# Where the row work of the last matrix product runs: three moves in the tail of a hybrid decoder block on one Trainium2 core

## The chip, the cores and the metric

The kernel runs on one core of a Trainium2 chip. The metric is device time in microseconds (us) of one execution; three executions of the kernel before gave 1152.98, 1154.11 and 1154.29, median 1154.11. Engine names are those of the profile: PE multiplies matrices, DVE and ACT work on elements and rows, POOL is the general-purpose engine (GpSimd), and SP only issues DMA transfers here.

## The reference

One decoder layer in float32 on 1024 tokens of width 1024. Everything but the last two lines is left alone by the change:

```python
n = _rmsnorm(h, pre_mix_gain[l])
...                                     # two groups of heads, mixed into h
h = h + _rmsnorm(mix, post_mix_gain[l])
n2 = _rmsnorm(h, pre_ffn_gain[l])
gu = jnp.einsum('bsd,df->bsf', n2, w_ffn_in[l])
ff = jax.nn.silu(gu[..., :D_FF]) * gu[..., D_FF:]
ff = jnp.einsum('bsf,fd->bsd', ff, w_ffn_out[l])      # the down product, D_FF = 2816
h = h + _rmsnorm(ff, post_ffn_gain[l])                # the row work
```

The row work of a token is the sum of squares of its 1024 results, one reciprocal root from it, and `h + ff * root * gain`.

## The kernel before, in words

The last stage, the down product, multiplies 2816 inner values for 1024 tokens and 1024 columns. It is cut into halves both ways (a Strassen-like scheme), so that seven half-size products take the place of eight. They run in the order p = 1, 2, 6, 5, 7, 3, 4. Each goes through 11 steps j (`NJ`), each step through four token tiles i of 128, and each tile takes three matmuls of 128x512, because float32 values are split into a high and a low part: `dah`/`dal` for the activations, `dwh`/`dwl` for the weights (`mm3`, lines 118 to 120). One step is 12 matmuls.

While step n runs, the operands of step n+4 (`AHEAD`) are prepared. `down_load` lets SP load 128x512 of weights (`dwr`) and of activations (`dar`), 256 KB each. `down_split` makes the high part on ACT (line 114) and the low part on DVE (line 115), for both. All of these tiles have four buffers. The high part of step n+4 is written where that of step n stood, so ACT waits until PE is through with n; and the load of `dar` for n+4 goes where that of n stood, so it waits for the DVE's subtraction of n.

The product's results come in tiles of 128 tokens by 512 columns. `PAIRS` names four pairs of token tiles (t0, t1); pair i keeps its partial results in `parts`: c11 and c12 are the two column halves of t0, c22 the second half of t1, and the first half of t1 is what the PSUM bank dA holds after p = 4. c11 is complete after p = 2, c22 after p = 7, c12 after p = 3.

The row work stands in three helpers. `row_tiles` loads the 128x1024 rows of h (`ht`, 512 KB). `square` sums the squares of a half on ACT and multiplies it by the gain into `y`. `ffn_tail` gets the root through DVE and POOL (`rstd2`, lines 100 and 102), adds `y` times root to `ht` on DVE (line 1149, two halves), and lets SP store each half (line 1151). All of it is written in p = 4. The t0 tiles of the pairs stand in steps 0 to 3, with the gain multiplication on POOL; the rows of t1 are loaded in steps 3 to 6 into the four buffers that t0 used.

The last four steps of p = 4 (`late`) are turned round: tile by tile, steps 7 to 10 of it, so that the tiles of t1 come to an end one after the other, and each one's row work follows (`after`).

The program's text does not fix where an instruction stands on its engine. A scheduler places instructions by when it expects them to be ready, for each engine, and the engine then takes them strictly in that order. SP's queue is such an order too: a transfer that waits holds up the ones behind it.

Of the kernel before, what the change touches and what calls it, by code (L numbers as in the profile page):

```python
# [7 lines left out]
F32 = mybir.dt.float32  # L8
F32R = mybir.dt.float32r
AF = mybir.ActivationFunctionType  # L10
ALU = mybir.AluOpType
PSUM = bass.MemoryType.PSUM

P = 128
S = 1024
D = 1024
NT = S // P
# [12 lines left out]
PAIRS = [(0, 6), (1, 7), (2, 4), (3, 5)]  # L30
# [18 lines left out]
def hybrid_block(ctx: ExitStack, tc: tile.TileContext, io: dict, out: bass.AP):  # L49
# [1081 lines left out]
    def row_tiles(t):  # L1131
        ht = po.tile([P, D], F32, tag="ht", name=f"ht_{t}", bufs=4)
        nc.sync.dma_start(out=ht, in_=h_d[t * P:(t + 1) * P, :])
        rows[t] = ht, small(2, "sq"), po.tile([P, D], F32, tag="y", name=f"y_{t}", bufs=4)

    def square(t, dh, src, eng):
        ht, ss, y = rows[t]
        cs = slice(dh * 512, dh * 512 + 512)
        s = po.tile([P, 512], F32, tag="junk", name=f"junk_{t}_{dh}", bufs=2)
        nc.scalar.activation(s, src, AF.Square, scale=D ** -0.5, accum_out=ss[:, dh:dh + 1])  # L1140
        eng.tensor_tensor(out=y[:, cs], in0=src, in1=gpo[:, cs], op=ALU.mult)  # L1141

    def ffn_tail(t):
        ht, ss, y = rows[t]
        ts = slice(t * P, (t + 1) * P)
        r = rstd2(ss)
        for dh in range(2):
            cs = slice(dh * 512, dh * 512 + 512)
            nc.vector.scalar_tensor_tensor(out=ht[:, cs], in0=y[:, cs], scalar=r, in1=ht[:, cs],
                                           op0=ALU.mult, op1=ALU.add)  # L1150
            nc.sync.dma_start(out=out[ts, cs], in_=ht[:, cs])
# [6 lines left out]
    def after(p, i):  # L1158
# [14 lines left out]
        elif p == 3:  # L1173
            nc.vector.tensor_tensor(out=parts["c12", i], in0=c, in1=parts["c12", i], op=ALU.add)
        else:
            square(t1, 0, a, nc.vector)
            ffn_tail(t1)
# [4 lines left out]
    for p in (1, 2, 6, 5, 7, 3, 4):  # L1182
# [4 lines left out]
        if p == 4:  # L1187
            for i in range(4):
                row_tiles(PAIRS[i][0])
        late = range(NJ - 4, NJ) if p == 4 else range(0)  # L1190
        for j in range(NJ):
# [11 lines left out]
            if p == 4 and j < 4:  # L1203
                t0, t1 = PAIRS[j]
                for dh in range(2):
                    square(t0, dh, parts[("c11", "c12")[dh], j], nc.gpsimd)
                ffn_tail(t0)
            if p == 4 and 3 <= j < 7:
                t1 = PAIRS[j - 3][1]
                row_tiles(t1)  # L1210
                square(t1, 1, parts["c22", j - 3], nc.gpsimd)
# [48 lines left out]
```

## Time and profile before

| What | Value |
|---|---|
| median of three executions | 1154.11 us |
| the profiled execution: its own time | 1152.77 us |
| the profiled execution: span in the trace | 1151.0 us |
| PE busy | 1110.7 us, 96% of the span |
| DVE, ACT, POOL busy | 723.1, 512.3, 176.8 us |
| p = 4, first to last matmul start | 1103.23 to 1142.12 us |
| last matmul start to the end of the span | 8.9 us |

The span is counted from the first to the last thing in the trace; the execution's own time is 1.77 us longer. All positions are microseconds from the span's start. An engine that is idle costs nothing by itself: what counts is which wait ends last.

### The profile page before, as it was taken

The page shows a single profiled execution, that of the slowest core. Times are in us where ns is not written, and L with a number is a line of the kernel's source. Part 1 is how long each engine was busy: PE and PEld are TensorE (multiplying, and loading weights), DVE is VectorE, ACT ScalarE, POOL GpSimd, SP SyncE. Part 2 cuts the span into 40 slices and gives each one's busy share as a digit, 9 for nine tenths or more (in the row PEclk, how much of TensorE's full clock was granted, in tenths as well). Part 3 has the DMA queues.
Part 4 walks back from the last instruction along what each step waited for, and adds up shares of the span by engine and source line. Part 5 has one row for each costly group of instructions (what it writes and reads, how often), then busy time and mean ns, then how long its engine had stood idle before and what let it go on. Part 6 is the DMA issues. An engine that isn't in the chain of part 4 may idle for free.

```text
span 1151.0 us, 15645 instructions
## 1 busy us (share of the span) xinstructions
PE 1110.7 (96%) x5421; PEld 917.1 (80%) x5421; DVE 723.1 (63%) x1288; ACT 512.3 (45%) x989; POOL 176.8 (15%) x247
## 2 busy tenths in 40 slices
PE   8999999999999989979999999999999999999995
PEld 7988777888877768758888888888888888888883
DVE  5565434677779667688766576666665454644575
ACT  5443324565567434364333333333333334444561
POOL 3032113343347231100000000000000000200041
PEclk9999999999999999989999999999999999999997
DMA  7120214233345364356574557455654587666664
GB/s 262 60 92 2 83 64 120 83 93 119 75 120 174 115 232 148 110 183 237 204 253 148 181 185 240 161 183 183 230 169 141 198 302 224 196 191 196 197 199 172
DMA packets 85953, 187.76 MB, mean 163 GB/s; under 512 B 9905, under 2 KB 28401, under 8 KB 83058
## 3 DMA queue, kind: packets, MB, share of 16 engines
q1 hardware_dynamic: 85874, 186.76, 49.8%
q8 instruction: 43, 0.70, 0.2%
q14 instruction: 36, 0.29, 0.1%
HBM read 128.76 MB, written 49.58 MB: 155 GB/s over the span
## 4 chain that ended last, share of the span: by engine, by line
PE 58%; DVE 2%; issue 1%; POOL 1%; DMA 1%; ACT 1%; DVEq 0%; POOLq 0%; SPq 0%; ACTq 0%
PE guA L118 7%; PE guA L119 7%; PE guA L120 7%; PE guC L120 4%; PE guC L119 4%; PE guC L118 4%; PE dA L118 3%; PE dA L120 3%; PE dA L119 3%; PE dC L118 3%; PE dC L119 3%; PE dC L120 3%; PE guE L118 2%; PE guE L119 2%; PE guE L120 2%; PE mx L120 2%
## 5 line engine op out<-in xcount | busy, mean ns | idle before, releaser
L1141 POOL TENSOR_TENSOR y<-c,gpo 128x512 f32<-128x512 f32 x12 | 20.5, 1734 | 610.2 <-DMA dwr<-ws_d 490.5
L115 DVE TENSOR_TENSOR dal<-dar,dah 128x512 fp32r<-128x512 f32 x77 | 56.4, 733 | 88.2 <-ACT dah L114 88.2
L114 ACT CAST dah<-dar 128x512 fp32r<-128x512 f32 x77 | 48.0, 623 | 104.3 <-PE dC L119 45.8
L119 PE MATMUL dA<-dwl,dah 128*128 128x512 f32 x176 | 70.1, 398 | 2.9 <-DVE dwl L115 2.9
L118 PE MATMUL dA<-dwh,dah 128*128 128x512 f32 x176 | 69.9, 397 | 2.3 <-ACT dah L114 2.3
L120 PE MATMUL dA<-dwh,dal 128*128 128x512 f32 x176 | 69.7, 396 | 0.0
L473 POOL TENSOR_SCALAR sm<-cb,csq 128x128 f32<-128x128 f32 (+3 forms) x64 | 50.3, 787 | 90.2 <-PE pt L508 77.5
L497 ACT ACTIVATE sm<-sm,st 128x128 f32<-128x128 f32 (+3 forms) x64 | 50.0, 781 | 27.7 <-DVE st L493 27.4
L115 DVE TENSOR_TENSOR ptl<-pt,pth 128x512 fp32r<-128x512 f32 (+2 forms) x96 | 51.7, 553 | 10.4 <-ACT pth L114 9.8
L115 DVE TENSOR_TENSOR dwl<-dwr,dwh 128x512 fp32r<-128x512 f32 x77 | 55.4, 720 | 3.2 <-ACT dwh L114 3.2
L114 ACT CAST pth<-pt 128x512 fp32r<-128x512 f32 (+2 forms) x96 | 43.7, 477 | 27.6 <-PE pt L508 27.3
L115 DVE TENSOR_TENSOR fbc_1l<-ts,fbc_1h 128x1024 fp32r<-128x1024 f32 x22 | 26.9, 1225 | 45.9 <-ACT fbc_1h L114 45.9
L118 PE MATMUL qk<-nth,qkw 128*128 128x512 f32 x128 | 53.5, 419 | 0.5 <-DVE k L115 0.4
L118 PE MATMUL mx<-woh,mh 128*128 128x512 f32 x128 | 51.3, 401 | 2.5 <-ACT mh L114 2.5
L491 PE MATMUL s<-k,qu 128*128 128x384 f32 (+4 forms) x192 | 51.1, 365 | 1.5 <-DVE st L493 1.3
L120 PE MATMUL mx<-woh,ml 128*128 128x512 f32 x128 | 50.5, 397 | 1.2 <-DVE ml L115 1.2
L118 PE MATMUL dC<-dwh,dah 128*128 128x512 f32 x132 | 51.3, 389 | 0.0
L119 PE MATMUL dC<-dwl,dah 128*128 128x512 f32 x132 | 51.3, 389 | 0.0
L120 PE MATMUL dC<-dwh,dal 128*128 128x512 f32 x132 | 51.3, 389 | 0.0
L947 ACT COPY u<-guA 128x512 f32<-128x512 f32 x44 | 25.8, 585 | 56.7 <-PE guA L120 56.7
L120 PE MATMUL qk<-nth,qkw 128*128 128x512 f32 x128 | 50.5, 395 | 0.1
L119 PE MATMUL qk<-ntl,qkw 128*128 128x512 f32 x128 | 50.4, 394 | 0.0
(742 smaller groups left out, 3278.6 us busy)
## 6 DMA issues: line engine op xcount, KB each, us to landing
graw<-in_w_gu SPq DMA_DIRECT2D x22, 1024.0 KB, 5.4
wj<-in_w_ffn_out SPq DMA_DIRECT2D x22, 512.0 KB, 4.5
aj<-ff_d SPq DMA_DIRECT2D x22, 512.0 KB, 3.8
dar<-as_d SPq DMA_DIRECT2D x44, 256.0 KB, 3.5
dwr<-ws_d SPq DMA_DIRECT2D x44, 256.0 KB, 3.7
dwr<-in_w_ffn_out SPq DMA_DIRECT2D x33, 256.0 KB, 3.6
dar<-ff_d SPq DMA_DIRECT2D x33, 256.0 KB, 4.2
ws_d<-wx SPq DMA_DIRECT2D x11, 512.0 KB, 4.3
```

The source lines that it names most:

```text
L114: nc.scalar.copy(out=hi, in_=src)
L115: (lo_eng or nc.vector).tensor_tensor(out=lo, in0=src, in1=hi.bitcast(F32), op=ALU.subtract)
L118: nc.tensor.matmul(o, ah, bh, start=first, stop=False, **kw)
L119: nc.tensor.matmul(o, ah, bl, start=False, stop=False, **kw)
L120: nc.tensor.matmul(o, al, bh, start=False, stop=last, **kw)
L473: nc.gpsimd.tensor_scalar(out=sm[:, :n], in0=cbs[hh][:, :n], scalar1=csq[:, hh * NT + i:hh * NT + i + 1], scalar2=1.0, op0=ALU.add, op1=AL ...
L491: nc.tensor.matmul(o[:, :w], qu[:, hl, ts], ks_[hh][:, ks], start=hl == 0, stop=hl == 1)
L497: nc.scalar.activation(sm[:, :n], sm[:, :n], AF.Exp, bias=m, scale=-1.0, accum_out=ssum)
L947: nc.scalar.copy(out=s, in_=o)
L1141: eng.tensor_tensor(out=y[:, cs], in0=src, in1=gpo[:, cs], op=ALU.mult)
```

## The change

Four things are done to the row work; the products stay as they are.

- Each half's squares and gain multiplication are written where the half is complete: c11 in p = 6, c22 in p = 3, c12 in p = 4. The result of the multiplication is kept in place of the half, so only the first half of t1 still needs a `y` tile.
- The gain multiplication is done by DVE everywhere; POOL keeps only the root.
- The rows `ht` have eight buffers in place of four and are loaded in p = 6 and p = 3; the sums of squares have a tile for each token tile.
- The stores of the t0 rows are written one step later than their row work (`tail_store`), and the row work of a t1 tile behind the squares of the next.

```diff
@@ -1129,26 +1129,32 @@
     rows = {}
 
     def row_tiles(t):
-        ht = po.tile([P, D], F32, tag="ht", name=f"ht_{t}", bufs=4)
+
+        ht = po.tile([P, D], F32, tag="ht", name=f"ht_{t}", bufs=NT)
         nc.sync.dma_start(out=ht, in_=h_d[t * P:(t + 1) * P, :])
-        rows[t] = ht, small(2, "sq"), po.tile([P, D], F32, tag="y", name=f"y_{t}", bufs=4)
-
-    def square(t, dh, src, eng):
-        ht, ss, y = rows[t]
-        cs = slice(dh * 512, dh * 512 + 512)
+        rows[t] = ht, po.tile([P, 2], F32, tag="ssq", name=f"ssq_{t}", bufs=NT), {}
+
+    def square(t, dh, src, y):
+        ht, ss, ys = rows[t]
         s = po.tile([P, 512], F32, tag="junk", name=f"junk_{t}_{dh}", bufs=2)
         nc.scalar.activation(s, src, AF.Square, scale=D ** -0.5, accum_out=ss[:, dh:dh + 1])
-        eng.tensor_tensor(out=y[:, cs], in0=src, in1=gpo[:, cs], op=ALU.mult)
-
-    def ffn_tail(t):
-        ht, ss, y = rows[t]
-        ts = slice(t * P, (t + 1) * P)
+        nc.vector.tensor_tensor(out=y, in0=src, in1=gpo[:, dh * 512:dh * 512 + 512], op=ALU.mult)
+        ys[dh] = y
+
+    def tail_store(t):
+        for dh in range(2):
+            cs = slice(dh * 512, dh * 512 + 512)
+            nc.sync.dma_start(out=out[t * P:(t + 1) * P, cs], in_=rows[t][0][:, cs])
+
+    def ffn_tail(t, store=True):
+        ht, ss, ys = rows[t]
         r = rstd2(ss)
         for dh in range(2):
             cs = slice(dh * 512, dh * 512 + 512)
-            nc.vector.scalar_tensor_tensor(out=ht[:, cs], in0=y[:, cs], scalar=r, in1=ht[:, cs],
+            nc.vector.scalar_tensor_tensor(out=ht[:, cs], in0=ys[dh], scalar=r, in1=ht[:, cs],
                                            op0=ALU.mult, op1=ALU.add)
-            nc.sync.dma_start(out=out[ts, cs], in_=ht[:, cs])
+        if store:
+            tail_store(t)
 
     def down_step(o, p, j, i, fresh):
         w, a = down["w", p, j][1], down["a", p, j][1]
@@ -1173,8 +1179,11 @@
         elif p == 3:
             nc.vector.tensor_tensor(out=parts["c12", i], in0=c, in1=parts["c12", i], op=ALU.add)
         else:
-            square(t1, 0, a, nc.vector)
-            ffn_tail(t1)
+            square(t1, 0, a, po.tile([P, 512], F32, tag="y", name=f"y_{t1}", bufs=4))
+            if i > 0:
+                ffn_tail(PAIRS[i - 1][1])
+            if i == 3:
+                ffn_tail(t1)
 
     NJ = NF // 2
     cbank = {}
@@ -1184,9 +1193,6 @@
         if p in (2, 5):
             cbank = {i: bank(CTAGS[i], f"dC{p}_{i}") for i in range(4)}
         banks = ABANK if p in (1, 6, 7, 4) else cbank
-        if p == 4:
-            for i in range(4):
-                row_tiles(PAIRS[i][0])
         late = range(NJ - 4, NJ) if p == 4 else range(0)
         for j in range(NJ):
             if j in late:
@@ -1200,15 +1206,19 @@
                 act_job(NJ - 1)
                 act_sums(NJ - 1)
             n += 1
-            if p == 4 and j < 4:
-                t0, t1 = PAIRS[j]
-                for dh in range(2):
-                    square(t0, dh, parts[("c11", "c12")[dh], j], nc.gpsimd)
-                ffn_tail(t0)
-            if p == 4 and 3 <= j < 7:
-                t1 = PAIRS[j - 3][1]
-                row_tiles(t1)
-                square(t1, 1, parts["c22", j - 3], nc.gpsimd)
+            if p in (6, 3, 4) and 1 < j < 6:
+                t0, t1 = PAIRS[j - 2]
+                if p == 6:
+                    row_tiles(t0)
+                    square(t0, 0, parts["c11", j - 2], parts["c11", j - 2])
+                elif p == 3:
+                    row_tiles(t1)
+                    square(t1, 1, parts["c22", j - 2], parts["c22", j - 2])
+                else:
+                    square(t0, 1, parts["c12", j - 2], parts["c12", j - 2])
+                    ffn_tail(t0, False)
+            if p == 4 and 2 < j < 7:
+                tail_store(PAIRS[j - 3][0])
         for i in range(4):
             for j in late:
                 down_step(banks[i], p, j, i, False)
```

First place: SP's queue near the end of p = 4. `dwr_9` and `dar_9` are the loads of step 9 (ahead of the longer number stands the step). Before, the rows of the t0 tiles are ht_10419, 10423, 10427, 10431, in the order of the pairs, and those of t1 follow with the loads of `ht`:

```order
L1151 DMA out<-ht_10423 128x512
L1066 DMA dwr_9_10637<-ws_d 128x512
L1151 DMA out<-ht_10423 128x512
L1133 DMA ht_10587<-h_d 128x1024
L1151 DMA out<-ht_10427 128x512 x2
L1151 DMA out<-ht_10431 128x512
L1133 DMA ht_10618<-h_d 128x1024
L1151 DMA out<-ht_10431 128x512
L1066 DMA dar_9_10641<-ff_d 128x512
L1133 DMA ht_10649<-h_d 128x1024
L1066 DMA dwr_10_10668<-ws_d 128x512
L1066 DMA dar_10_10672<-ff_d 128x512
```

The same place now; the t0 rows are ht_9399, 9429, 9459, 9489:

```order
L1066 DMA dwr_8_10595<-ws_d 128x512
L1147 DMA out<-ht_9399 128x512
L1066 DMA dar_9_10634<-ff_d 128x512
L1066 DMA dwr_9_10630<-ws_d 128x512
L1147 DMA out<-ht_9399 128x512
L1147 DMA out<-ht_9429 128x512
L1066 DMA dwr_10_10665<-ws_d 128x512
L1066 DMA dar_10_10669<-ff_d 128x512
L1147 DMA out<-ht_9429 128x512
L1147 DMA out<-ht_9459 128x512 x2
L1147 DMA out<-ht_9489 128x512 x2
```

Before, all eight stores of t0 and two loads of `ht` stood ahead of `dar_9`; now one store does, and three stand ahead of the loads of step 10. The loads of `ht` are gone from here: all eight stand among the loads for the end of p = 1 and for p = 2, where four of them stood before.

Second place: DVE in p = 4, from the third t0 tile to the low parts of step 9 or 10. Before:

```order
L1149 SCALAR_TENSOR_TENSOR ht_10427<-y_10430,st_322_10543,ht_10427 128x512
L115 TENSOR_TENSOR dwl_6_10526<-dwr_6_10523,dwh_6_10525 128x512
L115 TENSOR_TENSOR dal_6_10530<-dar_6_10527,dah_6_10529 128x512
L1149 SCALAR_TENSOR_TENSOR ht_10427<-y_10430,st_322_10543,ht_10427 128x512
L1149 SCALAR_TENSOR_TENSOR ht_10431<-y_10434,st_324_10581,ht_10431 128x512
L115 TENSOR_TENSOR dwl_7_10564<-dwr_7_10561,dwh_7_10563 128x512
L115 TENSOR_TENSOR dal_7_10568<-dar_7_10565,dah_7_10567 128x512
L1149 SCALAR_TENSOR_TENSOR ht_10431<-y_10434,st_324_10581,ht_10431 128x512
L115 TENSOR_TENSOR dal_8_10613<-dar_8_10610,dah_8_10612 128x512
L115 TENSOR_TENSOR dwl_8_10609<-dwr_8_10606,dwh_8_10608 128x512
```

Now:

```order
L1141 TENSOR_TENSOR c_9621<-c_9621,gpo 128x512
L115 TENSOR_TENSOR dal_7_10567<-dar_7_10564,dah_7_10566 128x512
L115 TENSOR_TENSOR dwl_7_10563<-dwr_7_10560,dwh_7_10562 128x512
L1154 SCALAR_TENSOR_TENSOR ht_9459<-c_9051,st_318_10612,ht_9459 128x512
L1154 SCALAR_TENSOR_TENSOR ht_9459<-c_9619,st_318_10612,ht_9459 128x512
L115 TENSOR_TENSOR dal_8_10602<-dar_8_10599,dah_8_10601 128x512
L115 TENSOR_TENSOR dwl_8_10598<-dwr_8_10595,dwh_8_10597 128x512
L100 TENSOR_SCALAR st_319_10645<-ssq_9491 128x1
L1154 SCALAR_TENSOR_TENSOR ht_9489<-c_9053,st_320_10647,ht_9489 128x512
L1154 SCALAR_TENSOR_TENSOR ht_9489<-c_9621,st_320_10647,ht_9489 128x512
L115 TENSOR_TENSOR dal_9_10637<-dar_9_10634,dah_9_10636 128x512
L115 TENSOR_TENSOR dwl_9_10633<-dwr_9_10630,dwh_9_10632 128x512
```

The additions of the t0 rows stay among the low parts and stand about one step later than before; four gain multiplications (one is the first row shown) have come in between.

Third place: DVE's end, the row work of the first two t1 tiles, now:

```order
L1141 TENSOR_TENSOR y_10691<-dA_8767,gpo 128x512
L100 TENSOR_SCALAR st_321_10711<-ssq_10249 128x1
L1154 SCALAR_TENSOR_TENSOR ht_10247<-y_10691,st_322_10713,ht_10247 128x512
L1154 SCALAR_TENSOR_TENSOR ht_10247<-c_9891,st_322_10713,ht_10247 128x512
L1141 TENSOR_TENSOR y_10707<-dA_8768,gpo 128x512
L100 TENSOR_SCALAR st_323_10735<-ssq_10279 128x1
L1154 SCALAR_TENSOR_TENSOR ht_10277<-y_10707,st_324_10737,ht_10277 128x512
L1154 SCALAR_TENSOR_TENSOR ht_10277<-c_9893,st_324_10737,ht_10277 128x512
```

Apart from where the second addition reads its half, these are the instructions of before in the order of before: the row work of one tile still ends before that of the next begins, though the text interleaves them. On PE, only the last steps differ: before, the three matmuls of step 10 for the first tile stood scattered among those of the second; now each tile's twelve stand together.

## Rows read from the trace of the kernel before

**Rows 1.** The page: span and instructions.

```profile
span 1151.0 us, 15645 instructions
```

**Rows 2.** Timeline of PE, p = 4: start, duration, line, operation [idle before, what ended it].

```profile
1103.23 0.39 PE L118 MATMUL dA<-dwh,dah 128*128 128x512 f32 x1
...
1119.55 0.39 PE L118 MATMUL dA<-dwh,dah 128*128 128x512 f32 x1
...
1122.98 0.39 PE L118 MATMUL dA<-dwh,dah 128*128 128x512 f32 x1
1126.30 0.79 PE L119 MATMUL dA<-dwl,dah 128*128 128x512 f32 x1 [2.93 <-DVE dwl L115]
...
1129.84 0.80 PE L118 MATMUL dA<-dwh,dah 128*128 128x512 f32 x1 [2.32 <-ACT dah L114]
...
1142.12 0.39 PE L120 MATMUL dA<-dwh,dal 128*128 128x512 f32 x1
```

**Rows 3.** Busy time by stretch: PE, PEld, DVE, ACT, POOL, then clock, DMA share, GB/s.

```profile
1130.00:1135.00 5.00, 5.00 (x12) 3.94 (x13) 1.84 (x3) 1.23 (x2) 0.00 (x0) 0.50 0.31 125
```

**Rows 4.** The chain that ended last: start, duration, what.

```profile
1122.28 1.71 DVE ht L1149
1124.00 0.33 SPq L1151
...
1124.39 4.75 DMA dar<-ff_d
...
1129.16 0.63 ACT dah L114
...
1142.86 0.13 DVE st L100
```

**Rows 5.** Timeline of DVE: row work and low parts.

```profile
1072.43 1.89 DVE L1172 TENSOR_TENSOR c<-c,u 128x512 f32<-128x512 f32 x3
...
1101.14 0.69 DVE L115 TENSOR_TENSOR dal<-dar,dah 128x512 fp32r<-128x512 f32 x1 [1.42 <-ACT dah L114]
...
1102.35 2.48 DVE L1174 TENSOR_TENSOR c<-dC,c 128x512 f32<-128x512 f32 x4
...
1106.14 1.78 DVE L115 TENSOR_TENSOR dal<-dar,dah 128x512 fp32r<-128x512 f32 x1
...
1117.79 0.75 DVE L1149 SCALAR_TENSOR_TENSOR ht<-y,st,ht 128x512 f32<-128x512 f32 x1 [1.73 <-POOL st L102]
...
1136.57 0.69 DVE L1141 TENSOR_TENSOR y<-dA,gpo 128x512 f32<-128x512 f32 x1 [3.41 <-ACT junk L1140]
...
1144.97 0.69 DVE L1141 TENSOR_TENSOR y<-dA,gpo 128x512 f32<-128x512 f32 x1
...
1146.44 1.42 DVE L1149 SCALAR_TENSOR_TENSOR ht<-y,st,ht 128x512 f32<-128x512 f32 x2 [0.66 <-POOL st L102]
```

**Rows 6.** Timeline of POOL, p = 4.

```profile
1103.12 5.96 POOL L1141 TENSOR_TENSOR y<-c,gpo 128x512 f32<-128x512 f32 x4 [113.73 <-DVE c L1174]
...
1117.21 1.06 POOL L102 TENSOR_TENSOR st<-st,mhalf 128x1 f32<-128x1 f32 x2
```

**Rows 7.** Timeline of ACT: high parts and squares.

```profile
1100.48 0.62 ACT L114 CAST dah<-dar 128x512 fp32r<-128x512 f32 x1 [1.58 <-PE dC L119]
1101.01 0.61 ACT L114 CAST dwh<-dwr 128x512 fp32r<-128x512 f32 x1
...
1135.85 0.60 ACT L1140 ACTIVATE junk<-dA 128x512 f32<-128x512 f32 x1 [3.42 <-PE dA L120]
...
1142.61 0.60 ACT L1140 ACTIVATE junk<-dA 128x512 f32<-128x512 f32 x1 [2.03 <-PE dA L120]
```

**Rows 8.** Busy time by stretch, p = 1.

```profile
945.00:950.00 5.00, 5.00 (x23) 4.13 (x22) 2.48 (x4) 2.28 (x4) 0.00 (x0) 1.00 0.91 333
```

**Rows 9.** DMA issues of 940 to 956: KB each, us to landing.

```profile
dar<-ff_d SPq DMA_DIRECT2D x7, 256.0 KB, 4.4
...
ht<-h_d SPq DMA_DIRECT2D x3, 512.0 KB, 5.4
```

## The prediction, made before the changed kernel ran

> **What bounds the kernel now.** I read the page first, then the timeline of PE over the last product, then the chain that ended last, then the timelines of the other engines around the places the chain names. The reader should see that PE sets the time almost everywhere and loses it in one place. The profiled span is 1151.0 us [rows 1]. In p = 4 PE starts at 1103.23 and runs one step of 12 matmuls in 2.72 us: step 6 starts at 1119.55, so 72 matmuls took 16.32 us, 0.2267 us each [rows 2]. At this pace all 132 matmuls of p = 4 would have started by 1103.23 + 131 x 0.2267 = 1132.92. The last one starts at 1142.12 instead [rows 2], 9.2 us late. PE stops twice: 2.93 us for the low weights of step 8 on DVE, and 2.32 us for the high activations of step 9 on ACT [rows 2]. Then it runs at a granted clock of 0.50 [rows 3], the lower level of 1.2 GHz, so the 5.25 us of idle time cost 9.2 in the end, 1.75 us for each.
>
> The chain says why. A DVE addition to a t0 row begun at 1122.28 takes 1.71 us, SP can issue its store only at 1124.00, and the load of step 9's activations stands behind it in SP's queue: issued at 1124.39, it is on its way for 4.75 us, and ACT casts it at 1129.16 [rows 4]. I take that addition to be slow because POOL multiplies beside it: a low part takes 0.69 us alone, and 1.78 at 1106.14 [rows 5] while POOL's four multiplications run from 1103.12 for 5.96 us [rows 6].
>
> After the last matmul, DVE finishes the four t1 tiles one by one. Their multiplications start at 1136.57 and, three tiles later, at 1144.97 [rows 5], so a tile takes 2.80 us, a little more than PE needs for its 12 matmuls. The last one ends at 1146.44 + 1.42 = 1147.86 [rows 5]; the last store and the end of the program take the remaining 3.14 us.
>
> **Part one, POOL's multiplications go to DVE.** What remains on POOL is the root (two take 1.06 us [rows 6]). A gain multiplication with both inputs and its output in SBUF is not in this trace on DVE, but an addition of that form, also in place, is: three take 1.89 us, 0.69 each and 0.60 from start to start [rows 5]. I price the multiplication at 0.60. In p = 6 and p = 3 four of them (2.4 us) and four squares on ACT (0.72 us with the reading of the sum, as from 1135.85 to DVE's start at 1136.57 [rows 5, 7]; 2.9 us) are added in some ten steps of 2.72. They are hidden by the four buffers: operands are made four steps, 10.9 us, ahead, and ACT and DVE each work about 2.4 of every 5 us in such a stretch [rows 8]. If that cover were gone they would cost PE at most their own 2.9 us.
>
> **Part two, DVE in p = 4.** Here the cover is thin, so I followed the order shown above from the last free moment. The four additions to c12 end at 1102.35 + 2.48 = 1104.83 [rows 5]; they were not slowed by POOL. From there to the low parts of step 9, DVE has 14 low parts and 4 multiplications at 0.60, 8 additions to `ht` at 0.67 (the second of a pair, 1.42 - 0.75 [rows 5]), and 4 short operations at 0.13 [rows 4]: 10.8 + 5.4 + 0.5 = 16.7 us. To this come the waits for the root: from the multiplication at 1144.97 to the addition at 1146.44 are 1.47 us [rows 5], of which 0.60 are the multiplication, so a root takes 0.87 from its short operation to the addition. A multiplication stands in between for three rows, which leaves 0.14 at two of them; the fourth waits 0.74 in full. The sum is 17.7, so step 9's low parts are done at 1122.55.
>
> Step 10 can't be split earlier than that in any case. Its buffer is freed by step 6, whose matmuls end the step at 1122.27. In steady state ACT's high activations start 0.03 before a step's end and the high weights 0.53 later (1100.48 and 1101.01, where a step ends at 1103.23 - 2.72 = 1100.51 [rows 2, 7]), and the low part starts 0.66 after the first of them (1101.14 [rows 5]). So DVE starts step 10 at 1122.90 and ends at 1124.20. In the tile-by-tile part PE wants step 10's low weights for the first tile 10 matmuls after 1122.27, at 1124.54. The slack is 0.35 us on DVE and 0.34 on PE, 0.69 together. PE does not stop.
>
> **Part three, stores and loads on SP.** The loads of steps 9 and 10 wait for the low parts of steps 5 and 6. By the same count step 5's are done near 1110.6 and step 6's near 1114.0, and the stores ahead of them wait for additions that end before those. The last load leaves near 1114.2, at a landing time of 4.4 us [rows 9] it is there by 1118.6, and ACT wants it at 1122.2: 3.6 us to spare. The loads of `ht` that crowded this place are gone.
>
> They go to p = 1, where DMA is at 0.91 already [rows 8]. Loads of 256 KB land in 4.4 us there, those of 512 KB in 5.4 [rows 9], and PE does not wait. A load is issued when the low part four steps before is done, about 1.3 us into a step, and wanted 10.88 - 1.3 = 9.5 us later. Four more loads of 512 KB make the crowding last longer, not deeper, so I price them at nothing; the other end is 2.1 MB at 333 GB/s [rows 8], 6.3 us, all of it put on one load: 4.4 + 6.3 - 9.5 = 1.2 us of idle, at 1.75 each 2.1 us.
>
> **Part four, the interleaved t1 tiles.** DVE's order is that of before, so this part is worth nothing. But the chain starts from a better place: the first tile's last matmul starts at 1103.23 + 95 x 0.2267 = 1124.76, ACT takes it 0.49 later (1142.12 to 1142.61 [rows 2, 7]), DVE 0.72 after that, at 1125.97. Three tiles of 2.80 bring the last to 1134.37; PE alone would allow 1132.92 + 1.21 = 1134.13. Before, it was 1144.97.
>
> **The sum.** 1144.97 - 1134.37 = 10.6 us: 9.2 from PE and 1.4 from the tile chain that trailed behind it. What follows is unchanged, so the span falls to 1140.4. The execution's own time, 1152.77, would be 1142.2; it is 1.3 us below the median of the runs, 1154.11, from which I get **1143.5 us**.
>
> **The rivals.**
>
> *The root holds the multiplication up.* DVE's multiplications of p = 4 read two SBUF tiles while POOL takes a root, and POOL's multiplications did slow such work. If either makes the other wait for its whole length, each of three rows loses about 0.45 us: 1.35 - 0.69 = 0.7 us, time 1144.2. Against it: the addition at 1117.79 takes 0.75 [rows 5] beside the second of the two roots from 1117.21 on [rows 6], its price alone. The Trainium skill, page "SBUF — State Buffer", section "Who interferes with whom", has it as a rule that a DVE instruction with two SBUF inputs and a GpSimd instruction that reads SBUF exclude each other for the whole instruction; it makes no exception for short ones. By that rule the sum would be the 1144.2 of this rival; for the large multiplications the trace agrees, for the root that one row does not.
>
> *The slack is too small.* My count of DVE has 17.7 us and 0.69 to spare. If it is 2 us worse than that slack allows, PE stops for 2 us and pays 1.75 for each: 1143.5 + 3.5 = 1147.0.
>
> *The loads of the rows crowd p = 1.* The upper end above: 1145.6.
>
> *The change doesn't do what it says.* Three stores still stand ahead of step 10's loads. If they held them up as before, PE's waits would stay and the time would be 1154. Against it: the last of them waits for the third of the eight additions, near 1112.8, before the low part of step 6 that its load needs anyway; before, it was the eighth addition that held SP.
>
> *Slower.* The dear price of DVE belongs to the row work itself, in-place or beside PE and DMA at full load, and not to POOL. Then 4 multiplications and 8 additions in p = 4 take 1.78 in place of 0.60 and 0.67: 4 x 1.18 + 8 x 1.11 = 13.6 us, less 0.69, a stop of 12.9 us even without the lower clock, time 1156.4 or more. It decides from (10.6 + 0.69) / 12 = 0.94 us of extra time per operation. Against it: the four additions at 1102.35, partly beside POOL but with one input from PSUM, kept their 0.6, the in-place additions at 1072.43, far from any work of POOL, too, and the low part at 1.78 lies beside POOL's multiplications [rows 5, 6].
>
> **How the numbers follow.** The forecast has 0.70, its own range being 1142 to 1145; the root 0.07; the small slack 0.11; the crowding 0.05; no effect 0.03; slower 0.04. The first four are faster by more than 0.2% (2.3 us, about what a measurement of this kernel can tell from no change): 0.93. The range 1141.7 to 1148.0 takes in those four, from the profiled execution's own level less half a microsecond up to a small slack that fails by 2.5 us, and leaves out the last two with some of the tails.
>
> **What would show it.** Right: PE's matmuls of p = 4 without idle time from 1103 to about 1133, granted clock 1.00 until then; POOL with roots alone in p = 4; no DVE operation of 128x512 above 0.8 us; low parts of step 9 done before ACT has step 10's high part; the last DVE addition near 1137. Wrong: PE idle in front of step 9 or 10 with DVE's low part as the releaser (slack), with a load as the releaser (stores, or p = 1 if it comes earlier), or DVE work of 128x512 near 1.8 us with POOL at rest.

## The result and the profile after

The changed kernel takes 1145.13 us (median of six executions, 1143.87 to 1146.01); the kernel before, beside it on the same chip, 1154.20. The ratio is 0.9924, with a 95% interval from 0.9911 to 0.9936. The prediction was 1143.5. The profiled execution took 1143.87, its span is 1142.2 us.

The timeline of PE in p = 4 answers to [rows 2]:

```profile
1103.97 0.39 PE L118 MATMUL dA<-dwh,dah 128*128 128x512 f32 x1
...
1124.37 0.39 PE L118 MATMUL dA<-dwh,dah 128*128 128x512 f32 x1
1124.73 0.50 PE L119 MATMUL dA<-dwl,dah 128*128 128x512 f32 x1
1125.07 0.39 PE L120 MATMUL dA<-dwh,dal 128*128 128x512 f32 x1
1125.30 0.40 PE L118 MATMUL dA<-dwh,dah 128*128 128x512 f32 x1
1125.94 0.50 PE L119 MATMUL dA<-dwl,dah 128*128 128x512 f32 x1 [0.24 <-DVE dwl L115]
...
1134.44 0.39 PE L120 MATMUL dA<-dwh,dal 128*128 128x512 f32 x1
```

Both long stops are gone. What remains are two small waits, each in front of a matmul with low weights, one in step 9 and one in step 10: 0.36 and 0.64 from start to start where 0.23 is usual. The matmul behind each starts 0.34 later, as at 1125.07. The last matmul starts at 1134.44, 30.47 after the first; without any wait it would be 131 x 0.2267 = 29.70. Those four gaps make up the difference of 0.77.

The busy times of two stretches answer to [rows 3, 8]. The clock of TensorE is 1.00, its upper level of 2.4 GHz, where it was 0.50 before, and in p = 1 PE is busy all the time although DMA now stands at 0.94:

```profile
945.00:950.00 5.00, 5.00 (x24) 4.14 (x23) 2.15 (x4) 2.24 (x4) 0.00 (x0) 1.00 0.94 340
...
1130.00:1135.00 5.00, 4.83 (x22) 3.67 (x20) 3.54 (x8) 0.88 (x5) 1.10 (x2) 1.00 0.57 210
```

The timelines of DVE and POOL in p = 4 answer to [rows 5, 6]:

```profile
1108.68 0.68 DVE L1141 TENSOR_TENSOR c<-c,gpo 128x512 f32<-128x512 f32 x1
1109.81 0.75 DVE L1154 SCALAR_TENSOR_TENSOR ht<-c,st,ht 128x512 f32<-128x512 f32 x1 [0.44 <-POOL st L102]
...
1116.25 0.69 DVE L1141 TENSOR_TENSOR c<-c,gpo 128x512 f32<-128x512 f32 x1
1116.85 0.69 DVE L115 TENSOR_TENSOR dal<-dar,dah 128x512 fp32r<-128x512 f32 x1
1117.45 0.69 DVE L115 TENSOR_TENSOR dwl<-dwr,dwh 128x512 fp32r<-128x512 f32 x1
1118.58 1.42 DVE L1154 SCALAR_TENSOR_TENSOR ht<-c,st,ht 128x512 f32<-128x512 f32 x2 [0.44 <-POOL st L102]
...
1121.11 0.21 DVE L100 TENSOR_SCALAR st<-ssq 128x1 f32<-128x1 f32 x1
1122.05 1.42 DVE L1154 SCALAR_TENSOR_TENSOR ht<-c,st,ht 128x512 f32<-128x512 f32 x2 [0.73 <-POOL st L102]
...
1124.59 0.69 DVE L115 TENSOR_TENSOR dal<-dar,dah 128x512 fp32r<-128x512 f32 x1
...
1127.42 0.69 DVE L1141 TENSOR_TENSOR y<-dA,gpo 128x512 f32<-128x512 f32 x1 [1.54 <-ACT junk L1140]
...
1136.02 0.69 DVE L1141 TENSOR_TENSOR y<-dA,gpo 128x512 f32<-128x512 f32 x1
...
1137.56 0.75 DVE L1154 SCALAR_TENSOR_TENSOR ht<-y,st,ht 128x512 f32<-128x512 f32 x1 [0.73 <-POOL st L102]
1138.22 0.74 DVE L1154 SCALAR_TENSOR_TENSOR ht<-c,st,ht 128x512 f32<-128x512 f32 x1
```

```profile
1108.91 0.86 POOL L102 TENSOR_TENSOR st<-st,mhalf 128x1 f32<-128x1 f32 x1 [616.07 <-DVE st L100]
1112.69 0.86 POOL L102 TENSOR_TENSOR st<-st,mhalf 128x1 f32<-128x1 f32 x1 [2.92 <-DVE st L100]
1116.48 2.06 POOL L102 TENSOR_TENSOR st<-st,mhalf 128x1 f32<-128x1 f32 x1 [2.93 <-DVE st L100]
1121.47 0.55 POOL L102 TENSOR_TENSOR st<-st,mhalf 128x1 f32<-128x1 f32 x1 [2.92 <-DVE st L100]
```

No operation of DVE in p = 4 is stretched any more. But look at POOL: the same root of 128x1 takes 0.55 us when DVE rests, 0.86 beside one multiplication, and 2.06 beside three operations in a row (1116.25, 1116.85 and 1117.45). It ends at 1118.54, 0.40 after the last of the three (1117.45 + 0.69 = 1118.14). In each of three rows DVE then waits 0.44 us for it, in the fourth 0.73. Step 10's low part starts at 1124.59 the moment DVE is through with step 9's: DVE is late by a little, and PE's two waits are that.

### The profile page after: what moved, and what is told of

It is laid out like the page before. It is cut to its first block, busy times and chain, and to the rows that moved or that the text cites. A ratio compares the mean times of both kernels' runs of the same rounds, so it can differ in the third digit from the quotient of the medians.

```text
span 1142.2 us, 15633 instructions
## 1 busy us (share of the span) xinstructions
PE 1107.8 (97%) x5421; PEld 915.4 (80%) x5421; DVE 724.0 (63%) x1300; ACT 512.4 (45%) x989; POOL 158.8 (14%) x235
## 4 chain that ended last, share of the span: by engine, by line
PE 60%; DVE 2%; ACT 1%; issue 0%; POOL 0%; DMA 0%; POOLq 0%; DVEq 0%; SPq 0%; ACTq 0%
PE guA L118 7%; PE guA L120 7%; PE guA L119 7%; PE guC L120 4%; PE guC L119 4%; PE guC L118 4%; PE dA L119 3%; PE dA L120 3%; PE dA L118 3%; PE dC L120 3%; PE dC L119 3%; PE dC L118 3%; PE guE L118 2%; PE guE L119 2%; PE guE L120 2%; PE mx L120 2%
## 5 line engine op out<-in xcount | busy, mean ns | idle before, releaser
L115 DVE TENSOR_TENSOR dal<-dar,dah 128x512 fp32r<-128x512 f32 x77 | 53.2, 691 | 83.2 <-ACT dah L114 83.2
L102 POOL TENSOR_TENSOR st<-st,mhalf 128x1 f32<-128x1 f32 x16 | 10.9, 682 | 668.2 <-DVE st L100 668.2
L115 DVE TENSOR_TENSOR dwl<-dwr,dwh 128x512 fp32r<-128x512 f32 x77 | 52.9, 687 | 2.1 <-ACT dwh L114 2.1
```

Of the source, the lines that this page charges most:

```text
L102: nc.gpsimd.tensor_tensor(out=r, in0=m, in1=mhalf, op=ALU.pow)
L115: (lo_eng or nc.vector).tensor_tensor(out=lo, in0=src, in1=hi.bitcast(F32), op=ALU.subtract)
```

## The experiments

The start of p = 1 shifts by some four us between profiled executions: 923.68 before, 924.42 after, 927.89 in the third experiment, and 926.61 in the eleventh, whose program is that of after. I therefore give two times beside the median: from the first matmul of p = 1 to the end of the span (which the page gives to a tenth), and from the first matmul of p = 4 to the end of the last row addition. The ratio is to the kernel before in the same series; experiments 5 to 8 ran on one chip, 1 to 4 and 9 to 11 on another. The first matmul of p = 4 comes 179.55 after that of p = 1 in every profiled execution, so what differs lies in the last two columns. They differ from each other in 3, 4 and 10, where the last store lands 2.5 us after its issue and not 2.1, so that the end comes half a microsecond later.

| Kernel | median us | ratio, 95% interval | p = 1 to end | p = 4 to last addition |
|---|---|---|---|---|
| before | 1154.20 | | 227.3 | 44.63 |
| after | 1145.13 | 0.9924, 0.9911 to 0.9936 | 217.8 | 34.99 |
| 1: before, multiplications on DVE | 1149.71 | 0.9957, 0.9942 to 0.9971 | 221.3 | 38.57 |
| 2: before, eight buffers, early loads | 1145.71 | 0.9932, 0.9912 to 0.9953 | 218.4 | 35.72 |
| 3: 1 and 2 together | 1145.84 | 0.9931, 0.9916 to 0.9946 | 218.1 | 34.76 |
| 4: after, multiplications on POOL | 1144.19 | 0.9926, 0.9904 to 0.9949 | 217.8 | 34.46 |
| 5: before, eight y buffers alone | 1152.17 | 0.9987, 0.9973 to 1.0 | 225.2 | 42.39 |
| 6: 2 with four y buffers | 1149.39 | 0.9962, 0.9948 to 0.9976 | 221.9 | 39.10 |
| 7: after, root on ACT | 1143.12 | 0.9907, 0.9892 to 0.9923 | 215.8 | 33.06 |
| 8: after, root begun earlier | 1143.54 | 0.9912, 0.9897 to 0.9926 | 216.4 | 33.71 |
| 9: after, t1 rows loaded in p = 4 | 1145.24 | 0.9933, 0.9916 to 0.9949 | 217.8 | 35.00 |
| 10: 7 with the constant | 1142.68 | 0.9909, 0.9894 to 0.9923 | 216.3 | 33.04 |
| 11: after, stores at once | 1146.36 | 0.9935, 0.9920 to 0.9949 | 217.7 | 34.98 |

### 1. Multiplications on DVE, nothing else

```diff
-                    square(t0, dh, parts[("c11", "c12")[dh], j], nc.gpsimd)
+                    square(t0, dh, parts[("c11", "c12")[dh], j], nc.vector)
...
-                square(t1, 1, parts["c22", j - 3], nc.gpsimd)
+                square(t1, 1, parts["c22", j - 3], nc.vector)
```

> The kernel before with one word changed at two places: all twelve gain multiplications of c11, c12 and c22 go from POOL to DVE, at the places where they stood; rows, loads and stores as before. My theory, two causes (the DVE lag comes from POOL's multiplications, which stretch DVE's operations and stand ahead of the root on POOL; the place of the row work and SP's order cost something of their own): DVE has no operation of 128x512 above 0.8 us, but two multiplications of c22 stand ahead of step 9's low parts and one more ahead of step 10's, 1.2 to 1.8 us that the slack of about 0.7 does not hold; step 10's activation load stands behind the eight t0 stores and three loads of rows. A stop of 1.5 to 2 us at step 9 or 10: 1147 to 1150. Rival A, POOL's multiplications are the whole cause: 1145 to 1146, as the kernel after. Rival B, SP's queue order is the whole cause: 1152 to 1154, with the two waits of before.

Measured: 1149.71, as my theory has it. PE still waits 0.3 us for DVE's low weights of step 9. A longer wait of PE, two pieces of the chain that ended last and a row of DVE show which stop is left:

```profile
PE dA L118 <- ACT dah L114: 1.6, 1, 1.6
```

```profile
1125.85 5.22 DMA dar<-ff_d
1131.16 0.63 ACT dah L114
```

```profile
1117.78 0.68 DVE L115 TENSOR_TENSOR dal<-dar,dah 128x512 fp32r<-128x512 f32 x1
```

The load is that of step 10. The low part of step 6, which frees its buffer, is done at 1118.46 (1117.78 + 0.68); the load leaves 7.4 us later, behind the stores and the loads of rows. So SP's order costs something even where no multiplication of POOL slows DVE.

### 2. Eight buffers and early loads, multiplications on POOL

```diff
-        ht = po.tile([P, D], F32, tag="ht", name=f"ht_{t}", bufs=4)
+        ht = po.tile([P, D], F32, tag="ht", name=f"ht_{t}", bufs=NT)
...
-        rows[t] = ht, small(2, "sq"), po.tile([P, D], F32, tag="y", name=f"y_{t}", bufs=4)
+        rows[t] = ht, po.tile([P, 2], F32, tag="ssq", name=f"ssq_{t}", bufs=NT), po.tile([P, D], F32, tag="y", name=f"y_{t}", bufs=NT)
...
+            if p == 3 and 3 <= j < 7:
+                row_tiles(PAIRS[j - 3][1])
```

(and the t0 stores one step later, by `tail_store`).

> The kernel before with eight row buffers, the t1 rows loaded in p = 3 and the t0 stores written a step later; the multiplications stay on POOL in p = 4. My theory, two causes: the low weights of step 8 are late on DVE because of POOL, so PE's first stop (2.9 us) stays; the loads of steps 9 and 10 go earlier than 1120, so the second stop (2.3 us, behind the late load) is gone, but DVE needs 1.2 us a step where PE wants one in 0.7, about 1 us of new waits on DVE. A stop of some 4 us in place of 5.25 at the same dear price: 1149 to 1152. Rival A, POOL's multiplications are the whole cause: 1153 to 1155. Rival B, SP's order is the whole cause: 1145 to 1147.

Measured: 1145.71, what I had given to rival B; my own theory, 1149 to 1152, failed. Before SP's order gets the credit, look at POOL in p = 4:

```profile
1105.01 5.96 POOL L1141 TENSOR_TENSOR y<-c,gpo 128x512 f32<-128x512 f32 x4 [21.94 <-DVE c L1179]
1110.93 1.06 POOL L102 TENSOR_TENSOR st<-st,mhalf 128x1 f32<-128x1 f32 x2
1116.93 1.07 POOL L102 TENSOR_TENSOR st<-st,mhalf 128x1 f32<-128x1 f32 x2 [4.94 <-DVE st L100]
```

The multiplications of c22 have left p = 4: with eight `y` buffers they no longer wait for the t0 rows. The experiment took away two things at once and does not tell them apart; experiments 5 and 6 do.

### 3. Both together, without the spreading in the text

The edits of 1 and 2, but stores at once:

```diff
-                    square(t0, dh, parts[("c11", "c12")[dh], j], nc.gpsimd)
+                    square(t0, dh, parts[("c11", "c12")[dh], j], nc.vector)
...
+            if p == 3 and 3 <= j < 7:
+                row_tiles(PAIRS[j - 3][1])
...
-                row_tiles(t1)
-                square(t1, 1, parts["c22", j - 3], nc.gpsimd)
+                square(t1, 1, parts["c22", j - 3], nc.vector)
```

> Both together in the kernel before, without the spreading in the text: multiplications on DVE, eight row buffers, t1 rows loaded in p = 3; results in y tiles, stores at once, no interleave. The scheduler itself takes the multiplications of c22 and c11 out of p = 4 once the row buffers no longer hold them back. My theory: the same as the kernel after, 1144.5 to 1146.0, with 12 low parts and additions of DVE in the same order. Rival (the places in the text or the results kept in place matter for themselves): 1147 or more.

Measured: 1145.84, 218.1 from p = 1 to the end, 34.76 from p = 4 to the last addition, 0.23 less than after. Neither the places of the multiplications in the text nor the results kept in place matter for themselves: once the buffers allow it, the scheduler puts the twelve multiplications where they stand in the kernel after, to a tenth of a microsecond from the start of p = 1. The squares on ACT it does not move: eleven of the twelve for c11, c12 and c22 stay in p = 4 here, four in the kernel after, and that costs nothing.

### 4. The kernel after, multiplications on POOL

```diff
-        nc.vector.tensor_tensor(out=y, in0=src, in1=gpo[:, dh * 512:dh * 512 + 512], op=ALU.mult)
+        eng.tensor_tensor(out=y, in0=src, in1=gpo[:, dh * 512:dh * 512 + 512], op=ALU.mult)
```

(`eng` is POOL for c11, c12 and c22, DVE for the first half of t1.)

> The kernel after with the multiplications of c11, c12 and c22 on POOL again, at their new places (eight in p = 6 and p = 3, four in p = 4). In p = 4 POOL multiplies only at the beginning: from 1103 to about 1109 two low parts and an addition are stretched by 0.9, 1.2 and 1.1 us, and four multiplications at 0.60 are gone from DVE, and with them the wait for the root is 0.9 at most; the sum up to step 9's low parts is 14 x 0.60 + 8 x 0.67 + 0.5 + 3.2 = 17.5 us, as in the kernel after. Theory, place counts and not the engine: 1144.5 to 1146.5. Rival A, any multiplication on POOL beside p = 4 costs as before (the roots behind the multiplications, 1.5 to 1.7 us of wait twice): 1148 to 1151. Rival B: in p = 1 and p = 3 too, where POOL's eight multiplications stretch low parts that PE then waits for: PE idle before 1103, span of p = 4 unchanged.

Measured: 1144.19, a little below the range of the theory, and 34.46 from p = 4 to the last addition: 0.53 less than on DVE. With 179.55 from p = 1 to p = 4, rival B falls too. The timeline of DVE shows the contention, early in p = 4, where it has time to make up for it:

```profile
1108.74 1.53 DVE L115 TENSOR_TENSOR dal<-dar,dah 128x512 fp32r<-128x512 f32 x1
...
1110.79 3.10 DVE L1154 SCALAR_TENSOR_TENSOR ht<-c,st,ht 128x512 f32<-128x512 f32 x3
```

So at these places the engine does not count. At the places of before it did: there the move to DVE alone took away 6.06 of the 44.63 (experiment 1). The first part of the change is one way to part of the gain, and is not needed where the multiplications stand early.

### 5 and 6. The two causes apart

Experiment 5 is the kernel before with one number changed:

```diff
-        rows[t] = ht, small(2, "sq"), po.tile([P, D], F32, tag="y", name=f"y_{t}", bufs=4)
+        rows[t] = ht, small(2, "sq"), po.tile([P, D], F32, tag="y", name=f"y_{t}", bufs=NT)
```

> The kernel before with one number changed: the result tiles y have eight buffers in place of four. The multiplications of c22 on POOL then no longer wait for the t0 rows and move out of p = 4; four multiplications stay at its beginning. SP's order is that of before: eight stores and two loads of rows ahead of step 9's activations. The start of p = 4 shifts from run to run by some us for reasons far ahead of it, so I count from the first matmul of p = 1 to the end of the span (before 227.3, after 217.8) as well. My theory, two causes (the four late POOL multiplications make DVE late for step 8; SP's order makes the load late for step 9): DVE does the last t0 addition 17.5 us after p = 4 begins, step 9's load is issued at 18.1, ACT casts at 23, PE wants it at 20.4: one stop of about 3 us before step 9, none before step 8; 221 to 224, time 1148 to 1151. Rival (with the late multiplications gone the order of SP no longer matters): 218 to 219, 1145 to 1146.5.

Experiment 6 is the second with the number back:

```diff
-        rows[t] = ht, po.tile([P, 2], F32, tag="ssq", name=f"ssq_{t}", bufs=NT), po.tile([P, D], F32, tag="y", name=f"y_{t}", bufs=NT)
+        rows[t] = ht, po.tile([P, 2], F32, tag="ssq", name=f"ssq_{t}", bufs=NT), po.tile([P, D], F32, tag="y", name=f"y_{t}", bufs=4)
```

> The kernel of the second experiment (eight row buffers, t1 rows loaded in p = 3, t0 stores a step later) with the y tiles back at four buffers, so that POOL's multiplications of c22 stand late in p = 4 again. My theory, two causes: SP's loads for steps 9 and 10 are early, but DVE reaches step 8's low weights some 22 us after p = 4 begins while PE wants them at 19.7: a stop of 2.5 to 3 us before step 8 and about 1 us more at steps 9 and 10, all with DVE's low part as the releaser; 221.5 to 224.5, time 1149 to 1151.5. Rival (SP's order is the whole cause): 218 to 219, 1145 to 1146.5.

Measured: 225.2 for the fifth (above the upper end of 224; its median of 1152.17 is above the expected 1151 as well, and the interval of its ratio reaches 1.0) and 221.9 for the sixth; both rivals fall. In the fifth PE waits once, for step 9's activations, whose load SP issues at 1124.76, 17.95 us after p = 4 begins at 1106.81 (18.1 expected). The buffer that it fills was free at 1117.08, after the low part of step 5 (1116.39 + 0.69), 7.7 us before. The granted clock falls to 0.50 behind the stop, and that is why one stop of 3.3 us costs more than I had put down. Its wait, the row of DVE, SP's queue and one stretch (PE, PEld, DVE, ACT, POOL, then clock, DMA share, GB/s):

```profile
PE dA L118 <- ACT dah L114: 3.3, 1, 3.3
```

```profile
1116.39 0.69 DVE L115 TENSOR_TENSOR dal<-dar,dah 128x512 fp32r<-128x512 f32 x1
```

```profile
1123.14 0.33 SPq L1133 DMA_DIRECT2D ht<-h_d  x1
1124.38 0.33 SPq L1151 DMA_DIRECT2D out<-ht  x1
1124.76 0.45 SPq L1066 DMA_DIRECT2D dar<-ff_d  x1
```

```profile
1132.00:1134.00 2.00, 2.00 (x6) 1.32 (x4) 0.25 (x1) 0.87 (x2) 0.00 (x0) 0.50 0.68 272
```

In the sixth the releaser is DVE, and the clock falls behind the stop too. Its waits of PE, one stretch, then POOL's late multiplications, then the DVE work beside them:

```profile
PE dA L119 <- DVE dwl L115: 3.1, 2, 2.9
```

```profile
1132.00:1134.00 2.00, 2.00 (x6) 1.47 (x5) 0.18 (x1) 0.37 (x1) 0.00 (x0) 0.50 0.03 8
```

```profile
1115.92 2.88 POOL L1141 TENSOR_TENSOR y<-c,gpo 128x512 f32<-128x512 f32 x1 [2.28 <-DVE ht L1153]
1119.50 1.28 POOL L1141 TENSOR_TENSOR y<-c,gpo 128x512 f32<-128x512 f32 x1 [0.69 <-DVE st L100]
1120.74 1.06 POOL L102 TENSOR_TENSOR st<-st,mhalf 128x1 f32<-128x1 f32 x2
```

```profile
1117.56 1.79 DVE L1153 SCALAR_TENSOR_TENSOR ht<-y,st,ht 128x512 f32<-128x512 f32 x1
...
1121.32 0.75 DVE L1153 SCALAR_TENSOR_TENSOR ht<-y,st,ht 128x512 f32<-128x512 f32 x1 [1.72 <-POOL st L102]
...
1125.72 1.78 DVE L1153 SCALAR_TENSOR_TENSOR ht<-y,st,ht 128x512 f32<-128x512 f32 x1
...
1128.03 1.75 DVE L115 TENSOR_TENSOR dwl<-dwr,dwh 128x512 fp32r<-128x512 f32 x1
```

The late multiplications do two things: beside the one at 1115.92 a DVE addition takes 1.79 in place of 0.75, and the one at 1119.50 keeps the roots behind it in POOL's queue, for which DVE waits 1.72. So each cause alone makes a stop: SP's order one before step 9, POOL's late multiplications one before step 8. From p = 4 to the last addition, moving the late multiplications alone takes away 2.24 of the 44.63 (experiment 5), changing SP's order alone 5.53 (experiment 6). Both gone, as in experiment 2, it is 8.91 of the 9.64 that the whole change brings.

### 7 and 8. The root

Experiment 7:

```diff
+    def rstd2a(ss):
+
+        q = small()
+        nc.scalar.activation(q, ss[:, 0:1], AF.Sqrt, bias=ss[:, 1:2])
+        r = small()
+        nc.vector.reciprocal(r, q)
...
-        r = rstd2(ss)
+        r = rstd2a(ss)
```

> The kernel after with another root in the row work of the down product: a square root on ACT with the second sum as its bias and a reciprocal on DVE, in place of DVE's short operation and POOL's power; the small constant under the root is left out. POOL has nothing to do in p = 4. If POOL's root is held up by DVE's two-input operations (in the profile after it takes 0.86, 0.86 and 2.06 us beside them and 0.55 alone, and DVE waits 0.44 us for it in three rows and 0.73 in the fourth): the waits of 0.44 are gone, DVE reaches step 9's low parts about 1 us earlier, PE has no small waits there, and the tail gets shorter by up to 0.7 us: 216 to 217.2 from p = 1 to the end against 217.8, time 1143.2 to 1144.5. Rival: the root is off the path, or ACT takes as long: 217.5 to 218.5, 1145; if ACT has to load its tables for each tile: 221 and more.

Experiment 8 (`first` for the second half of t0 and the first of t1):

```diff
+        if first:
+            ys["r"] = rstd2(ss)
         nc.vector.tensor_tensor(out=y, in0=src, in1=gpo[:, dh * 512:dh * 512 + 512], op=ALU.mult)
...
-        r = rstd2(ss)
+        r = ys["r"]
```

> The kernel after with the short operation ahead of the root written before the gain multiplication, so that POOL takes the root while DVE multiplies, and not after it. If POOL's root can run beside DVE's multiplication, the wait of 0.73 us of each t1 tile shrinks to 0.2, the tile chain is set by PE (2.72 a tile in place of 2.87), and the last tile ends 0.6 earlier: 216.8 to 217.3 from p = 1 to the end, 1144.1 to 1144.7. Rival, the one of the prediction (a two-input operation of DVE and POOL's root exclude each other for their whole length): the root begins only when the multiplication is done, the wait stays at 0.6 to 0.7: 217.6 to 218.0, 1145.

Measured: 215.8 and 216.4, both a little below their ranges. In the seventh PE has no wait at all in p = 4. From its first matmul to its last there are 29.70 us, which is the bound:

```profile
1106.69 0.39 PE L126 MATMUL dA<-dwh,dah 128*128 128x512 f32 x1
...
1136.39 0.39 PE L128 MATMUL dA<-dwh,dal 128*128 128x512 f32 x1
```

ACT loads its tables once, in 1.28 us early in p = 4; the square root takes 0.3 us and DVE's reciprocal 0.16. In the eighth, POOL's timeline, and a row of DVE, show the root in two settings:

```profile
1107.43 2.06 POOL L102 TENSOR_TENSOR st<-st,mhalf 128x1 f32<-128x1 f32 x1 [613.89 <-DVE st L100]
...
1119.99 2.06 POOL L102 TENSOR_TENSOR st<-st,mhalf 128x1 f32<-128x1 f32 x1 [2.92 <-DVE st L100]
1127.81 0.55 POOL L102 TENSOR_TENSOR st<-st,mhalf 128x1 f32<-128x1 f32 x1 [5.76 <-DVE st L100]
```

```profile
1127.58 0.68 DVE L1143 TENSOR_TENSOR y<-dA,gpo 128x512 f32<-128x512 f32 x1
```

The t0 rows multiply c12, which lies in SBUF like the gain: the root takes 2.06 or 0.86, and DVE still waits 0.44. The t1 rows multiply what stands in PSUM: beside such a multiplication, from 1127.58 on, the root takes 0.55, and the wait of 0.73 is gone. The rival named there is right for t0 and wrong for t1.

### 9 to 11. Loads, the constant, and nothing

Experiment 9 (the new lines stand behind `tail_store` in p = 4; in p = 3 the load is left out):

```diff
-        ht = po.tile([P, D], F32, tag="ht", name=f"ht_{t}", bufs=NT)
+        ht = po.tile([P, D], F32, tag="ht", name=f"ht_{t}", bufs=4)
...
+                t1 = PAIRS[j - 3][1]
+                ht = po.tile([P, D], F32, tag="ht", name=f"ht_{t1}", bufs=4)
+                nc.sync.dma_start(out=ht, in_=h_d[t1 * P:(t1 + 1) * P, :])
+                rows[t1] = ht, *rows[t1][1:]
```

> The kernel after with the rows of t1 loaded in p = 4 again, into the four buffers of the t0 rows; the multiplications stay spread over the products. SP's order has the loads of steps 9 and 10 behind one and three stores, the four loads of rows behind both. Theory (the place in SP's queue costs, not the loads themselves): 217.3 to 218.3 from the first matmul of p = 1 to the end, as the kernel after with 217.8; 1144.5 to 1146. Rival A (the loads in p = 3 crowd p = 3 and p = 4, so that their return helps): below 217.2. Rival B (rows in p = 4 are late for the tail or hold up steps 9 and 10 as before): above 219.5, 1147 and more.

Experiment 10, the seventh and in `square`:

```diff
+        if not ys:
+            b = po.tile([P, 1], F32, tag="ssb", name=f"ssb_{t}", bufs=NT)
+            nc.vector.tensor_scalar(out=b, in0=ss[:, dh:dh + 1], scalar1=RMS_EPS, scalar2=None, op0=ALU.add)
+            ys["b"] = 1 - dh, b
```

> The kernel after with the root on ACT as in the seventh experiment, but with the small constant: DVE adds it to the first of the two sums of a row as soon as that is there (p = 6 and p = 3), and the square root takes this as its bias. Eight operations of 128x1 on DVE, 0.13 us each, are added outside p = 4, where DVE works about half of the time. Theory: as the seventh experiment, 215.5 to 216.3 from p = 1 to the end, 1142.5 to 1143.8, faster than the kernel after by 1.5 to 2. Rival (the constant's absence made the chain shorter, or the added operations delay operands): 217 and more.

Experiment 11:

```diff
-                    ffn_tail(t0, False)
-            if p == 4 and 2 < j < 7:
-                tail_store(PAIRS[j - 3][0])
+                    ffn_tail(t0)
```

> The kernel after with the stores of a t0 row written at once again, right behind its additions. The scheduler builds from it the same order on every engine as from the kernel after, so it measures how far one program differs from itself: 217.4 to 218.2 from p = 1 to the end, 1144.3 to 1146. Anything outside this would mean that differences of that size tell nothing in the other runs.

Measured: 217.8, 216.3 and 217.7. In the ninth the loads of the rows stand behind those of steps 9 and 10 in SP's queue, and cost nothing. The tenth has the lowest median here, 2.4 us below after; up to the last addition it takes what the seventh takes (33.04 and 33.06). 216.3 is the upper end of what I expected, since the end comes 3.7 us after the last addition in place of 3.2. The eleventh missed its range for the median (1146.36, up to 1146 expected) but not for the other measure: medians of one program differ by 1.2 us here, the time from p = 4 to the last addition by 0.01. So the medians do not tell the kernel after from 2, 3, 4 and 9, which lie within 1.0 us of it; the last column tells more.

## Why the prediction was right, and where its sizes were off

**The mechanism.** Both stops go, PE runs at its upper clock, and the tiles of t1 follow: right. "PE does not stop" was not: one sign of being wrong, PE idle in front of step 10 with DVE's low part as the releaser, shows in small (0.24 at 1125.94), and 1145.13 lies just above the forecast's own range of 1142 to 1145. The sum was 10.6 us; from p = 4 to the last addition it was 44.63 - 34.99 = 9.64. The remaining 0.96 has a place: the first t1 tile's multiplication starts 23.45 after p = 4 begins, not 22.74 (0.71); three tiles take 2.87 each and not 2.80 (0.20), as DVE waits 0.73 for each root (1137.56) and not 0.66 [rows 5], for a reason that no run shows; the rest is 0.05. The difference of the medians holds more: p = 4 began 0.74 later in the profiled execution than before, ahead of anything that the change moves, which I had not allowed for; 0.96 and 0.74 are the 1.6 us between 1143.5 and 1145.13 but for 0.1. That it comes out so well is partly luck: the profiled execution lies 1.26 below its median, as before it lay 1.3 below, while two medians of one program lie 1.2 apart (experiment 11).

**The term that was too small** is part two's wait for the root, "which leaves 0.14 at two of them; the fourth waits 0.74 in full". Counted the same way, from the end of the operation ahead (a start plus 0.60) to the addition, it was 0.53 in three rows (1108.68 + 0.60 to 1109.81) and 0.81 in the fourth: 2.40 in place of 1.02. By that DVE was free for step 10 at 1124.59, 20.62 after p = 4 began, and not at 19.32: 1.30 late with 0.69 of slack, 0.61 over, and PE lost 0.77 (30.47 less 29.70). Experiment 7, without this wait, is at the bound of 29.70. This is the first rival, in cause and in size. It let either side wait, and put 0.45 on each of three rows, 1.35 in all; the three rows took 1.31 more than the sum had for them. Not the multiplication is held up, as its heading says, but the root, and DVE then waits for the root. I had given it 0.07. The row at 1117.79 [rows 5], on which I discounted it, is another case: two roots take 1.06 there from 1117.21 on [rows 6], so the second was under way when the addition began, and neither was slowed. The Trainium skill, page "SBUF — State Buffer", section "Who interferes with whom", says that a DVE instruction with two SBUF inputs contends with a GpSimd instruction that reads SBUF, and that one with at most one SBUF input, outside the modes that use two ports, does not; the roots of 2.06 and 0.55 in experiment 8 agree with both sentences.

**Part one** was priced rightly (0.60 from start to start, 1116.25 to 1116.85) and is not needed: experiment 4. **The slow addition** of the chain was put down to POOL's multiplications, by the row of the early ones of c12. The addition lies beside a late one, of c22:

```profile
1120.56 2.87 POOL L1141 TENSOR_TENSOR y<-c,gpo 128x512 f32<-128x512 f32 x1 [2.28 <-DVE ht L1149]
```

Experiment 6 shows the reason right for these, and experiment 4 that the early ones are covered. What I had not seen is the second price, the root behind a multiplication in POOL's queue: it was in the trace of before too, as the 1.73 in front of the addition at 1117.79 [rows 5].

**The late load** was taken to follow from the late additions. Experiment 5 shows that the order alone is enough: with no addition slowed the load of step 9 still leaves 17.95 us into p = 4, and the stop is 3.3 us. In **part three**, that the loads of `ht` cost nothing in p = 1 was right, with 179.55 from p = 1 to p = 4 before and after; by experiment 9 they cost nothing in p = 4 either, behind the operands' loads. **Part four** was right: the interleave changes no engine's order, and by experiment 11 the later stores change nothing.

**Idle time at 1.75 each** depends on what the clock does: 3.3 us cost 6.6 in experiment 5 (36.31 less 29.70 from first to last matmul), while 1.9 us cost 2.9 in experiment 1 (32.55 less 29.70), where the clock stays at 1.00. For the sum it did not matter, since all of it went.

Why p = 1 begins at different times, the traces show in part. Near 122 us, far ahead of the change, PE makes the same two waits of 1.4 and 0.3 us in every profiled execution. In experiments 1, 3, 5, 6, 7 and 11 the granted clock then falls to 0.50 for about three microseconds; in the seven others it stays at 1.00. One stretch of experiment 1, then the same of before:

```profile
122.20:125.40 3.20, 3.05 (x13) 2.96 (x14) 0.69 (x2) 1.14 (x3) 0.00 (x0) 0.50 0.01 5
```

```profile
122.20:125.40 3.20, 2.86 (x19) 2.36 (x20) 1.18 (x2) 2.02 (x6) 0.00 (x0) 1.00 0.06 26
```

Those six are the ones whose p = 1 begins latest, at 926.61 and after; 1.1 to 1.4 us of it are lost at this place, the rest between 350 and 510. After's 0.74 is lost near 500, where the clock stands at 0.50 from 497 to 507 and, before, only to 504.

What stays open is why the clock falls behind the same waits in one execution and not in the next, and why DVE's multiplication of a t1 tile waits for ACT's squares of the same bank; neither was tried.

## What to carry to other kernels

Look first at which buffers tie work to a place: eight in place of four let the scheduler move the multiplications by itself, and that, with the loads of t1's rows written in p = 3, brought what the rewritten text brought. A queue that serves two masters (SP with stores and operand loads, POOL with multiplications and roots) makes the later one wait for the slower. A tiny operation that waits for the busy engine is worth moving to an idle one: here the root on ACT gave 1.5 to 2 us.

## What the runs showed of the hardware that I had not expected

- A POOL operation of 128x1 took 0.55 us alone, 0.86 beside one DVE operation with two SBUF inputs, and 2.06 beside three in a row: it did not get in between them, and ended 0.40 after the last. Beside a DVE multiplication with one input from PSUM it took 0.55.
- TensorE's granted clock was at 0.50 (1.2 GHz) from 1130 to 1136 after one idle time of 3.3 us (experiment 5) and from 1132 to 1134 after one of 2.9 (experiment 6), but stayed at 1.00 (2.4 GHz) after one of 1.6 (experiment 1). Behind the same two waits of 1.4 and 0.3 us near 122 us it fell in six of the thirteen profiled executions and stayed in seven.
